# The last head of a differential-attention layer: the first output tile moved beside the first two score tiles, gates of that head kept on chip

## The chip, the cores and the metric

The kernel runs on one core of a Trainium2 chip. The metric is device time of one execution in microseconds (us). Three executions of the kernel before took 1778.83, 1778.11 and 1774.59 us; the median is 1778.11.

## What is computed

Two post-norm transformer layers over 1024 latent tokens of width 1024, with 256 context tokens as a prefix of the keys. Layer 0 is multi-head latent attention and is not touched. Layer 1 is differential attention with 8 heads: each head has two softmaxes over 1280 keys, and the second is taken off the first.

```python
def combine(o1, o2, gate):
    o = o1 - lam_full.astype(o1.dtype) * o2
    o = rms_norm(o, g_sub) * (1.0 - lambda_init)
    return gated(o, gate)                      # o * silu(gate)
...
o1, o1_c = prefix_attention(q[:, :, :, 0:1], k[:, :, :, 0], v, ...)
o2, o2_c = prefix_attention(q[:, :, :, 1:2], k[:, :, :, 1], v, ...)
...
x = layer_norm(DEEPNORM_ALPHA * x + gate[:, None, :] * (o @ out_w[i]), ln_g[i], ln_b[i])
```

The output is x after layer 1, so its projection with `out_w` and its LayerNorm end the kernel.

## The kernel before

Layer 1 works head by head, and each head in 8 row tiles of 128 tokens; one tile of one head is a step, written by `step1`. A step has three parts of three different tiles: the scores of tile t (`scores1`), the transposes of the combined probabilities of tile t-1 (`turn1`) and the values of tile t-2 (`values1`).

- `scores1` computes 128 x 1280 scores for both softmaxes in five PSUM banks of the eight ("b"), each by a pair of matmuls (L1347, L1348). DVE takes the negated maxima (`mx`, L1360 and L1364) and their minimum for each softmax (L1366). ACT writes the exponentials `p1` and `p0` (L1370), whose sums go through DVE (L1373 to L1375), and DVE combines both into one matrix (L1376).
- `turn1` transposes it on the PE (L1383, 4 + 4 + 2 blocks of 128) and splits each result into two fp16 parts: `ph` on ACT (L181), `pl` on DVE (L182).
- `values1` multiplies with the head's values in three passes (L1391 to L1393). ACT scales the result (L1396) and squares it (L1397), POOL makes the reciprocal root (L159, L160). For heads 0 to 6 POOL applies it (L1404) and SP stores the tile in DRAM, `o_d` (L1405). For the last head DVE multiplies by norm and gate in one instruction and writes the last 128 columns of `ws` (L1402).

Between these parts `step1` lets a second stream of PE work run, `side`, metered by five credits of a step (SLOT1, or SLOTO in the last head). PE's order is the written one (MAN1 is 'P'); the order of DVE, ACT, POOL and SP is made by a scheduler from readiness and priority. SP issues the DMAs and is one queue in order.

For heads 0 to 6 the second stream projects queries, keys, values and gates of the next head (`prod_q1`, `prod_k1`, `prod_v1`, `prod_w`). `prod_v1` ends by putting `top` on the list `later`: splitting the values, the SiLU of the gates in place and their store in DRAM, `sg_d`. Beside head 6 the stream is `v_last`: the projection of head 7's values and gates, interleaved with the preparation of `out_w`, whose eight blocks of 128 rows are kept as two fp32r parts each, `oHL`. `out_w1` prepares blocks 0 to 3; `out_pre` loads blocks 4 to 7 into `z` and `res` (L1450), scales the `res` ones on ACT (L1453) and all by the residual gate on POOL (L1454).

Head 7's second stream is the output projection. `out_open` loads ln_g into `wsq` (`gb2`), finishes the splits of blocks 4 to 7, and calls `out_load` for tiles 0 and 1. `out_load` brings a tile's 896 columns of heads 0 to 6 from `o_d` (L1482) and all its gates from `sg_d` (L1483), and POOL multiplies them (L1484). `out_turn` transposes blocks k = 0 to 6 of it (L1496) and splits them into `wx` (ACT, L176) and `wy` (DVE, L177); block 7 is there only after `values1`. `out_tile1` sums a tile in two banks, one for each half of 512 columns: 8 blocks of three matmuls (L185 to L187) each. The block k = 7 of both halves is last ("the close"); DVE adds the residual (L1531) and takes the statistics (L1532, L1535), POOL and ACT make the LayerNorm (L1545 to L1548; `wsq` is ln_g, `gb` ln_b), and SP stores the tile (L1549). The tile projected in step t is t-2. In steps 0 and 1 the second stream is empty, and two steps without scores follow step 7; I call them 8 and 9.

`w1(tag)` gives the next buffer of a tag: `ws` has three, `wx`, `wy`, `z` and `res` two, `wsq` one. A buffer that is given out again waits for the last reader of what it held.

Of the kernel before, what the change touches and what calls it, by code (L numbers as in the profile page):

```python
# [9 lines left out]
F32 = mybir.dt.float32  # L10
# [7 lines left out]
P = 128  # L18
# [17 lines left out]
NOW = 4  # L36
# [17 lines left out]
def hybrid_kernel(  # L54
# [994 lines left out]
    with ow_ctx, spool("o0") as op0:  # L1049
# [96 lines left out]
        for t in range(8):  # L1146
# [55 lines left out]
            "kr": ([P, NTOK], F32, 1), "kH": ([P, NTOK], F16, 1), "kL": ([P, NTOK], F16, 1)}  # L1202
    TAGV = {"rr": ([P, 512], F32, 1), "gg": ([P, SEQ // P, P], F32, 1), "Vf": ([P, NT, P], F32, 1)}

# [12 lines left out]
    oHL = [[wo4.tile([P, D], F32R, name=f"oH1{k}"), wo4.tile([P, D], F32R, name=f"oL1{k}")] for k in range(NOW)]  # L1217
    gate1 = wo4.tile([P, D], F32, name="gate1")
    wv1 = prv.enter_context(spool("a1projv", side="right"))
    for k_, v_ in TAGV.items():  # L1220
# [82 lines left out]
    def prod_v1(h):  # L1303
        w, uv = wt[1], un[1]
        gg, Vf = w1("gg"), w1("Vf")
        vt[h] = vh, vl = w1("vh"), w1("vl")
        vT = w1("rr")[:, :CTX]
# [26 lines left out]

        later.append(top)
        yield 0
# [50 lines left out]
    def values1(h, t, ph, pl, sm):  # L1387
# [11 lines left out]
        if h == H1 - 1:  # L1399
            oo, g = og[t]  # L1400
            c = slice(h * P, (h + 1) * P)
            dve.scalar_tensor_tensor(oo[:, c], o, ss[:, 1:2], g[:, c], op0=ALU.mult, op1=ALU.mult)  # L1402
            return
# [54 lines left out]
    def out_open():  # L1458

        prv.close()  # L1460
        wg1 = a1.enter_context(spool("a1outg"))
        place["g"] = wg1
        TAG1["g"] = ([P, D], F32, 2)
# [4 lines left out]
        out_load(0)  # L1468
        for k, w in enumerate(pre):
            if k % 2:  # L1470
                split(*oHL[NOW + k], w, e_lo=pool)
            else:
                act.activation(oHL[NOW + k][0], w, AF.Copy, scale=gsub)
                dve.scalar_tensor_tensor(oHL[NOW + k][1], w, gsub, fv(oHL[NOW + k][0]), op0=ALU.mult, op1=ALU.subtract)
            if k == 0:
                out_load(1)

    def out_load(t):

        ts = slice(t * P, (t + 1) * P)  # L1480
        o, g = og[t] = w1("ws"), w1("g")
        sp.dma_start(o[:, :DH], o_d[1][ts, :DH])  # L1482
        sp.dma_start(g, sg_d[1][ts, :])  # L1483
        pool.tensor_tensor(o[:, :DH], o[:, :DH], g[:, :DH], op=ALU.mult)  # L1484
# [3 lines left out]
    def out_turn(t, k0, n):  # L1488

        o, _ = og[t]  # L1490
        if k0 == 0:
# [15 lines left out]

    def out_tile1(t):

        ts = slice(t * P, (t + 1) * P)  # L1510
        tH, tL = oT[t]
        res = w1("res")
        sp.dma_start(res, zn_d[ts, :])
        y = [bank("b") for _ in range(2)]

        def mm(hh, k):
            c = slice(hh * 512, hh * 512 + 512)
            mm3(y[hh], tH[:, k, :], tL[:, k, :], oHL[k][0][:, c], oHL[k][1][:, c], k == 0, k == KT - 1)

        for hh in range(2):  # L1520
            for k in range(KT - 1):
                mm(hh, k)
                yield 1600
                if hh == 1 and k == 3:
                    out_turn(t, KT - 1, 1)
                    yield 256
        z, bs = w1("z"), w1("bs")
        for hh in range(2):
            mm(hh, KT - 1)
            c = slice(hh * 512, hh * 512 + 512)  # L1530
            dve.tensor_tensor(z[:, c], y[hh], res[:, c], op=ALU.add)  # L1531
            dve.bn_stats(bs[:, hh, :], z[:, c])  # L1532
# [31 lines left out]
    with tc.manual_schedule(engines={ENG[c] for c in MAN1}):  # L1564
# [38 lines left out]
        def v_last(h):  # L1603
            while later:
                later.pop(0)()
            out_early()
            yield from weave(prod_v1(h), chain(*[out_w1(k, lambda: w1("ws")) for k in range(NOW)],
                                               *[out_pre(k) for k in range(NOW, KT)]), range(1, 36, 2))

        g1 = gate_row1()  # L1610
        part = lambda h: (v for _, v in zip(range(4 if h else 0), g1))
        for h in range(H1):
# [5 lines left out]
            else:  # L1618
                while later:
                    later.pop(0)()  # L1620
                out_open()
            for t in range(SEQ // P):
                if last:
                    if t >= 2:
                        out_load(t)
                    G = weave(out_tile1(t - 2), out_turns(t - 1), (9, 12)) if t >= 2 else iter(())
                    if t == 2:
                        G = chain(out_turns(0), G)
                    credit[0] = 0
                step1((h, t), G, SLOT1 if not last else SLOTO)  # L1630
                if last:
                    for _ in G:
                        pass
            for _ in G:
                pass
        for t in range(SEQ // P - 2, SEQ // P):
            G = weave(out_tile1(t), out_turns(t + 1), (9, 12))
            credit[0] = 0
# [77 lines left out]
```

## Time and profile before

| | |
|---|---|
| median of three executions | 1778.11 us |
| profiled execution | 1777.68 us |
| its span in the profile | 1775.8 us (1.9 us lie around it) |
| mean granted clock of PE | 0.993 |
| PE busy | 1662.7 us, 94% |
| DVE, ACT, POOL busy | 69%, 63%, 46% |
| last head's steps 3 to 7 | 16.96 us each |

The span runs from the first to the last instruction, and times in the timelines count from its start. Head 7's first scores stand at about 1619 us, its last matmul ends at 1767, and the rest to 1775.8 is the last tile's LayerNorm and store. In a timeline a row has the start, the duration, the engine (SPq is SP's queue), the line, the operation, result and operands, and in brackets the idle time before it with what ended it. Rows of the waits give the total, how often and the longest. The granted clock is a share of full speed.

### The profile page before, as it was taken

Reading aid. Unit: us, or ns where it says so; the run is one execution under the profiler, and the core shown is the slowest. Engines: PE = TensorE matmul, PEld = TensorE weight load, DVE = VectorE, ACT = ScalarE, POOL = GpSimd, SP = SyncE. Lnnn points to the kernel's source line nnn. Section 1 sums busy time; section 2 is a strip of 40 time slices with the busy share of each in tenths; the row PEclk is TensorE's granted clock in tenths of the full one; section 3 lists DMA queues with packets and bytes.
Section 4 is the critical chain, followed back from the end, with each engine's and each line's share of the span. In section 5 each row is a group of like instructions: output and inputs, shape, how many; then the busy total and the mean of one; then the engine's idle time right before and its main releaser. Section 6 shows DMA issues by size and latency. Waiting matters only on the chain. (4 is left out here: it accounts for less than half of the span.)

```text
span 1775.8 us, 36794 instructions
## 1 busy us (share of the span) xinstructions
PE 1662.7 (94%) x14564; PEld 1232.4 (69%) x14564; DVE 1225.1 (69%) x2037; ACT 1117.2 (63%) x2235; POOL 822.2 (46%) x740
## 2 busy tenths in 40 slices
PE   7999999999999999899999999999999999988998
PEld 7999966556666565577867666767676757666876
DVE  7658675566665667646855778787877777878664
ACT  2551177677777777845635676767677766758542
POOL 1432147667777676846552323231414132455454
PEclk9999999999999999999999999999999999999999
DMA  8258520110111112155532213131312122241332
GB/s 302 85 151 258 165 69 22 41 45 21 42 46 28 37 55 69 57 176 187 166 101 61 78 54 80 55 81 55 79 43 69 41 57 62 66 127 67 109 111 71
DMA packets 111225, 154.84 MB, mean 87 GB/s; under 512 B 13415, under 2 KB 84679, under 8 KB 111054
## 3 DMA queue, kind: packets, MB, share of 16 engines
q1 hardware_dynamic: 102654, 144.90, 27.5%
q10 hardware_dynamic: 8400, 7.61, 1.3%
q8 instruction: 114, 1.87, 0.4%
q14 instruction: 57, 0.47, 0.1%
HBM read 98.65 MB, written 27.07 MB: 71 GB/s over the span
## 5 line engine op out<-in xcount | busy, mean ns | idle before, releaser
L779 POOL TENSOR_TENSOR pl<-p,ph 128x1024 f16<-128x1024 f32 (+1 forms) x176 | 365.4, 2082 | 150.0 <-ACT ph L778 123.4
L1370 ACT ACTIVATE p<-ps_b,mx 128x512 f32<-128x512 f32 (+1 forms) x384 | 230.2, 616 | 65.6 <-DVE mx L1366 64.6
L777 ACT ACTIVATE p<-ps_a,esc 128x1024 f32<-128x1024 f32 (+1 forms) x176 | 189.0, 1074 | 97.4 <-PE ps_a L835 91.3
L759 DVE TENSOR_REDUCE mx<-ps_a 128x1 f32<-128x1024 f32 x128 | 155.2, 1222 | 131.2 <-PE ps_a L757 131.1
L778 ACT CAST ph<-p 128x1024 f16<-128x1024 f32 (+1 forms) x176 | 177.1, 1006 | 5.5
L1364 DVE TENSOR_REDUCE mx<-ps_b 128x1 f32<-128x512 f32 x256 | 165.4, 680 | 0.4 <-PE ps_b L1348 0.3
L848 PE MATMUL ps_d<-Vh,pl 128*128 128x65 f16 x1344 | 146.6, 194 | 3.1 <-POOL pl L779 3.1
L845 PE MATMUL ps_d<-Vh,ph 128*128 128x65 f16 x1344 | 148.7, 195 | 0.0
L847 PE MATMUL ps_d<-Vl,ph 128*128 128x64 f16 x1344 | 147.5, 193 | 0.0
L845 PEld LDWEIGHTS <-ph 128*128 128x128 f16 x1344 | 123.7, 98 | 18.3 <-issue 5.2
L1347 PE MATMUL ps_b<-KS,QS 128*128 128x512 f16 (+1 forms) x384 | 126.5, 347 | 7.7 <-DVE pl L182 4.5
L847 PEld LDWEIGHTS <-ph 128*128 128x128 f16 x1344 | 124.3, 99 | 12.3 <-issue 0.5
L1395 POOL TENSOR_TENSOR sm<-sm,us 128x1 f32<-128x1 f32 x64 | 18.5, 288 | 245.9 <-DVE sm L1374 241.9
L833 PE MATMUL ps_a<-qH,KH 100*128 100x512 f16 x320 | 122.6, 383 | 9.1 <-ACT p L777 4.3
L1348 PE MATMUL ps_b<-KS,Q 128*128 128x512 f16 (+1 forms) x384 | 129.7, 347 | 0.0
L1383 PE MATMUL ps_b<-idr,p 128*128 128x128 f32 x640 | 102.7, 276 | 28.3 <-ACT rr L1313 7.8
L182 DVE SCALAR_TENSOR_TENSOR pl<-ps_b,lcf,ph 128x512 f16<-128x512 f32 (+1 forms) x192 | 116.8, 653 | 14.3 <-ACT ph L181 14.3
L848 PEld LDWEIGHTS <-pl 128*128 128x128 f16 x1344 | 123.5, 98 | 4.3 <-POOL pl L779 4.2
L181 ACT ACTIVATE ph<-ps_b,lcf 128x512 f16<-128x512 f32 (+1 forms) x192 | 115.4, 649 | 13.2 <-PE ps_b L1383 13.2
L834 PE MATMUL ps_a<-qH,KL 96*128 96x512 f16 x320 | 122.5, 383 | 0.0
L835 PE MATMUL ps_a<-qL,KH 96*128 96x512 f16 x320 | 121.9, 381 | 0.0
L1383 PEld LDWEIGHTS ps_b<-idr,p 128*128 128x128 f32 x640 | 77.0, 141 | 54.2 <-ACT p L1370 10.9
(438 smaller groups left out, 5293.6 us busy)
## 6 DMA issues: line engine op xcount, KB each, us to landing
ws<-in_dw SPq DMA_DIRECT2D x28, 512.0 KB, 4.1
adw<-in_ada_w SPq DMA_DIRECT2D x24, 512.0 KB, 4.7
adaw<-in_ada_w SPq DMA_DIRECT2D x16, 512.0 KB, 7.9
g<-sg_d SPq DMA_DIRECT2D x16, 512.0 KB, 9.1
sg_d<-gg ACTq DMA_DIRECT2D x40, 128.0 KB, 3.6
o_d<-op SPq DMA_DIRECT2D x7, 640.0 KB, 3.8
xt<-in_xT SPq DMA_DIRECT2D x16, 256.0 KB, 4.4
wgs<-in_w_in SPq DMA_DIRECT2D x32, 128.0 KB, 3.2
```

The source lines that it names most:

```text
L759: dve.tensor_reduce(mx[:, t, 0:1], ps, axis=AX.X, op=ALU.max)
L777: act.activation(p32[:, :n], st, AF.Exp, scale=esc0)
L778: act.copy(ph[:, :n], p32[:, :n])
L779: pool.tensor_tensor(pl[:, :n], p32[:, :n], ph[:, :n], op=ALU.subtract)
L845: pe.matmul(pv[:, t, :], ph[:, ts], Vh[:, k, h, :], start=(k == kcs[0] and t == 0), stop=False, skip_group_check=True)
L847: pe.matmul(pv[:, t, :V0], ph[:, ts], Vl[:, k, h, :], start=False, stop=False, skip_group_check=True)
L848: pe.matmul(pv[:, t, :], pl[:, ts], Vh[:, k, h, :], start=False, stop=(k == NT - 1), skip_group_check=True)
L1347: pe.matmul(out, qs[m][:, ts], ks[m][:, c0:c0 + n], start=True, stop=False)
L1348: pe.matmul(out, q1[m][:, ts], ks[m][:, c0:c0 + n], start=False, stop=True)
L1364: dve.tensor_reduce(mx[:, 2 + 2 * m + i:3 + 2 * m + i], b, axis=AX.X, op=ALU.max, negate=True)
L1370: act.activation(p[m][:, c0:c0 + n], b, AF.Exp, bias=nb, accum_out=sm[:, 2 + 3 * m + i:3 + 3 * m + i])
L1383: pe.transpose(st[:, j * P:(j + 1) * P], pc[:, (k0 + j) * P:(k0 + j + 1) * P], idn)
```

## The change

The changed file is longer, so lines move by 1 to 43; what was L1402 is L1408, L1366 is L1374, L1376 is L1384, L1404 and L1405 are L1410 and L1411, L1453 is L1459, L1482 to L1484 are L1496, L1499 and L1500, L1531 is L1570.

- Tile 0 is projected beside steps 0 and 1 of head 7: k = 0 to 3 of both halves in step 0, interleaved with the splits of `out_w` (`out_split`), k = 4 to 6 in step 1. Its two banks stay open until step 2.
- From step 2 on, the second half of tile s-2 and the first half of tile s-1 are computed, then the k = 7 transposes and close of tile s-2 (`out_step`, `out_close`). The transposes of tile s come behind that close.
- `out_first` loads tiles 0 and 1 in `v_last`, with gates in `wsq`; tile 0 is transposed at the end of `v_last`. ln_g takes `wsq` after them. Later tiles' gates go to the tag `gg`, which moves to a pool that stays.
- Head 7's values are split and its gates put through SiLU after step 1 (`out_gates`), into `g7` on chip. They aren't stored, and the loads of gates shrink to 896 columns.
- The credits of steps 0 and 1 are SLOTF.

```diff
 SLOTO = 0, 7000, 7000, 7000, 7000
+SLOTF = 0, 4800, 3200, 3200, 3200
...
@@ prod_v1
-        later.append(top)
+        if h < H1 - 1:
+            later.append(top)
+        else:
+            og.update(Vf=Vf, gg=gg, uv=uv)
@@ values1
-            dve.scalar_tensor_tensor(oo[:, c], o, ss[:, 1:2], g[:, c], op0=ALU.mult, op1=ALU.mult)
+            dve.scalar_tensor_tensor(og[t][:, DH:], o, ss[:, 1:2], og["g7"][:, t, :], op0=ALU.mult, op1=ALU.mult)
@@ out_load
-    def out_load(t):
+    def out_load(t, g_tag="gg"):
-        o, g = og[t] = w1("ws"), w1("g")
+        o, g = w1("ws"), w1(g_tag)
+        og[t] = o
         sp.dma_start(o[:, :DH], o_d[1][ts, :DH])
-        sp.dma_start(g, sg_d[1][ts, :])
+        sp.dma_start(g[:, :DH], sg_d[1][ts, :DH])
         pool.tensor_tensor(o[:, :DH], o[:, :DH], g[:, :DH], op=ALU.mult)
+    def out_gates():
+        vt[H1 - 1] = vh, vl = w1("vh"), w1("vl")
+        split16(vh, vl, og["Vf"], kc1)
+        prv.close()
+        wg1 = a1.enter_context(spool("a1outg", side="right"))
+        og["g7"] = wg1.tile(GG[0], GG[1], name="g7")
+        act.activation(flat(og["g7"]), flat(og["gg"]), AF.Silu, scale=og["uv"])
+    def out_mm(t, hh, ks):
+        for k in ks:
+            if k == 0:
+                oy[t, hh] = bank("b")
+            mm3(oy[t, hh], tH[:, k, :], tL[:, k, :], oHL[k][0][:, c], oHL[k][1][:, c], k == 0, k == KT - 1)
+            yield 1600
+    def out_step(s):
+        a, b = s - 2, s - 1
+        early, late_ = range(NOW), range(NOW, KT - 1)
+        if s == 0:
+            yield from weave(chain(out_mm(0, 0, early), out_mm(0, 1, early)), out_split(), (0, 2, 4, 6))
+            return
+        if s == 1:
+            yield from chain(out_mm(0, 0, late_), out_mm(0, 1, late_), out_turns(1))
+            return
...
+        if a:
+            yield from out_mm(a, 1, range(KT - 1))
+        if b <= end:
+            yield from out_mm(b, 0, early if a else range(KT - 1))
+        out_turn(a, KT - 1, 1)
+        yield 256
+        if a and b < end:
+            yield from out_mm(b, 0, late_)
+        yield from out_close(a, res)
+        yield from out_turns(s)
@@ v_last
             yield from weave(prod_v1(h), chain(*[out_w1(k, lambda: w1("ws")) for k in range(NOW)],
-                                               *[out_pre(k) for k in range(NOW, KT)]), range(1, 36, 2))
+                                               out_first(0), *[out_pre(k) for k in range(NOW, KT)],
+                                               out_first(1)), range(1, 36, 2))
+            yield from out_turns(0)
+        def out_first(t):
+            out_load(t, "wsq")
+            yield
```

What it does to the order of the queues stands below in three places. Numbers behind a name tell its uses apart.

First, SP's queue near the end of head 6, before: the stores and loads from the tiles in `o_d`, the last queries of head 7 (`QS`, `Q1`), then ln_b (`gb3`) and the blocks of `out_w`.

```order
L1482 DMA ws_3354_21996<-o_d1_100 128x896
L1482 DMA ws_3356_22003<-o_d1_100 128x896
L86 DMA QS0_3224_21118<-kH_3252_21275 64x512 x2
L86 DMA QS1_3225_21119<-kH_3252_21275 64x512
L86 DMA Q10_3222_21116<-kL_3253_21276 64x512 x2
L86 DMA QS1_3225_21119<-kH_3252_21275 64x512
L86 DMA Q11_3223_21117<-kL_3253_21276 64x512 x2
L1405 DMA o_d1_100<-o1_3272_21397 128x128
L966 DMA gb3_3254_21291<-in_ln_b 128x1024
L1450 DMA z_3305_21630<-in_out_w 128x1024
L1450 DMA res_3315_21691<-in_out_w 128x1024
```

The same place after:

```order
L1496 DMA ws_3305_21630<-o_d1_100 128x896
L1496 DMA ws_3351_21959<-o_d1_100 128x896
L1499 DMA wsq_3352_21960<-sg_d1_98 128x896
L87 DMA QS0_3224_21118<-kH_3252_21275 64x512 x2
L87 DMA Q10_3222_21116<-kL_3253_21276 64x512 x2
L87 DMA QS1_3225_21119<-kH_3252_21275 64x512 x2
L87 DMA Q11_3223_21117<-kL_3253_21276 64x512 x2
L967 DMA wsq_3359_22009<-in_ln_g 128x1024
L1411 DMA o_d1_100<-o1_3272_21397 128x128
L967 DMA gb3_3254_21291<-in_ln_b 128x1024
L1456 DMA z_3308_21652<-in_out_w 128x1024
L1456 DMA res_3323_21761<-in_out_w 128x1024
```

The load of tile 1's gates into `wsq` now stands ahead of the queries, and ln_g into the same `wsq` ahead of the store, of ln_b and of the blocks of `out_w`.

Second, POOL's queue at the same place, before: the last rotation work of head 7's queries (`rr`), then norms of head 6 (`ss`, `o1`) and the residual gate on `out_w`.

```order
L1245 TENSOR_TENSOR rr_3250_21269<-rr_3250_21269,rsw_3251_21270 128x512
L1395 TENSOR_TENSOR sm_3233_21153<-sm_3233_21153,us_2991_19668 128x1
L159 TENSOR_SCALAR ss_3274_21399<-ss_3274_21399 128x1
L160 TENSOR_TENSOR ss_3274_21399<-ss_3274_21399,neghalf_66 128x1
L1404 TENSOR_SCALAR o1_3272_21397<-o1_3272_21397,ss_3274_21399 128x128
L1395 TENSOR_TENSOR sm_3263_21318<-sm_3263_21318,us_2991_19668 128x1
L1454 TENSOR_TENSOR z_3305_21630<-z_3305_21630,gate1_12517 128x1024
L1454 TENSOR_TENSOR res_3315_21691<-res_3315_21691,gate1_12517 128x1024
```

After:

```order
L1249 TENSOR_TENSOR rr_3250_21269<-rr_3250_21269,rsw_3251_21270 128x512
L1500 TENSOR_TENSOR ws_3305_21630<-ws_3305_21630,wsq_3306_21631 128x896
L1403 TENSOR_TENSOR sm_3233_21153<-sm_3233_21153,us_2991_19668 128x1
L1500 TENSOR_TENSOR ws_3351_21959<-ws_3351_21959,wsq_3352_21960 128x896
L160 TENSOR_SCALAR ss_3274_21399<-ss_3274_21399 128x1
L161 TENSOR_TENSOR ss_3274_21399<-ss_3274_21399,neghalf_66 128x1
L1410 TENSOR_SCALAR o1_3272_21397<-o1_3272_21397,ss_3274_21399 128x128
L1403 TENSOR_TENSOR sm_3263_21318<-sm_3263_21318,us_2991_19668 128x1
L1460 TENSOR_TENSOR z_3308_21652<-z_3308_21652,gate1_12517 128x1024
L1460 TENSOR_TENSOR res_3323_21761<-res_3323_21761,gate1_12517 128x1024
```

The two products of tiles 0 and 1 (`ws`) come ahead of the norm whose result the store L1411 sends.

Third, DVE in one of the steps 3 to 7, from the statistics of an output tile (`bs`) on, before; `ws` is the normed and gated tile of head 7, `mx` the maxima.

```order
L1532 BN_STATS bs_3489_22775<-z_3488_22774 128x6 x2
L1364 TENSOR_REDUCE mx_3493_22804<-ps_b_3500_22826 128x1
L1535 BN_AGGR mv_3490_22786<-bs_3489_22775 128x2
L1360 TENSOR_REDUCE mx_3493_22804<-ps_b_3497_22808 128x2
L1364 TENSOR_REDUCE mx_3493_22804<-ps_b_3501_22830 128x1
L1364 TENSOR_REDUCE mx_3493_22804<-ps_b_3498_22814 128x1
L1366 TENSOR_SCALAR mx_3493_22804<-mx_3493_22804 128x1
L1364 TENSOR_REDUCE mx_3493_22804<-ps_b_3499_22818 128x1
L1366 TENSOR_SCALAR mx_3493_22804<-mx_3493_22804 128x1
L1402 SCALAR_TENSOR_TENSOR ws_3429_22419<-o1_3503_22869,ss_3505_22871,g_3430_22420 128x128
```

After:

```order
L1571 BN_STATS bs_3492_22799<-z_3491_22798 128x6 x2
L178 TENSOR_TENSOR wy_3495_22820<-ps_b_3496_22821,wx_3494_22819 128x512
L1574 BN_AGGR mv_3493_22810<-bs_3492_22799 128x2
L178 TENSOR_TENSOR wy_3495_22820<-ps_b_3497_22828,wx_3494_22819 128x384
L1372 TENSOR_REDUCE mx_3500_22843<-ps_b_3507_22865 128x1
L1368 TENSOR_REDUCE mx_3500_22843<-ps_b_3504_22847 128x2
L1372 TENSOR_REDUCE mx_3500_22843<-ps_b_3508_22869 128x1
L1372 TENSOR_REDUCE mx_3500_22843<-ps_b_3505_22853 128x1
L1374 TENSOR_SCALAR mx_3500_22843<-mx_3500_22843 128x1
L1372 TENSOR_REDUCE mx_3500_22843<-ps_b_3506_22857 128x1
L1408 SCALAR_TENSOR_TENSOR ws_3436_22458<-o1_3510_22908,ss_3512_22910,g7_22288 128x128
L1374 TENSOR_SCALAR mx_3500_22843<-mx_3500_22843 128x1
```

The splits `wy` of the next tile stand behind the statistics, and the write of `ws` (L1408, was L1402) stands ahead of the second negated maximum (L1374, was L1366), where before it stood behind both.

More of the change, by code (lines that the diff above doesn't have):

```diff
@@ L1218, in hybrid_kernel @@
     gate1 = wo4.tile([P, D], F32, name="gate1")
+    rot(wo4, GG[0], GG[1], "gg", GG[2], first=True)
+    place["gg"], TAG1["gg"] = wo4, GG
     wv1 = prv.enter_context(spool("a1projv", side="right"))
@@ L1305, in prod_v1 @@
         gg, Vf = w1("gg"), w1("Vf")
-        vt[h] = vh, vl = w1("vh"), w1("vl")
+        vh, vl = w1("vh"), w1("vl")
+        vt[h] = vh, vl
         vT = w1("rr")[:, :CTX]
@@ L1458, in out_open @@
     def out_open():
[L1460 to L1463, printed above, removed]
         og["gb2"] = w1("wsq")
@@ L1488, in out_turn @@
     def out_turn(t, k0, n):
-        o, _ = og[t]
+        o = og[t]
         if k0 == 0:
@@ L1506, in out_turns, with out_close @@
         yield 768
-    def out_tile1(t):
-        ts = slice(t * P, (t + 1) * P)
[L1511 to L1526, printed above, removed]
+    oy = {}
+    def out_mm(t, hh, ks):
+        tH, tL = oT[t]
+        c = slice(hh * 512, hh * 512 + 512)
+        for k in ks:
[12 more added lines that the diff above has]
+            return
+        res = w1("res")
+        sp.dma_start(res, zn_d[a * P:(a + 1) * P, :])
+        end = SEQ // P - 1
+        if a == end:
+            yield from out_mm(a, 0, late_)
+        if a:
[8 more added lines that the diff above has]
+        yield from out_turns(s)
+    def out_close(t, res):
+        ts = slice(t * P, (t + 1) * P)
         z, bs = w1("z"), w1("bs")
         for hh in range(2):
-            mm(hh, KT - 1)
+            for _ in out_mm(t, hh, (KT - 1,)):
+                pass
             c = slice(hh * 512, hh * 512 + 512)
-            dve.tensor_tensor(z[:, c], y[hh], res[:, c], op=ALU.add)
+            dve.tensor_tensor(z[:, c], oy[t, hh], res[:, c], op=ALU.add)
             dve.bn_stats(bs[:, hh, :], z[:, c])
@@ L1618, in hybrid_kernel @@
             else:
-                while later:
-                    later.pop(0)()
                 out_open()
@@ L1625, in hybrid_kernel @@
                         out_load(t)
-                    G = weave(out_tile1(t - 2), out_turns(t - 1), (9, 12)) if t >= 2 else iter(())
-                    if t == 2:
-                        G = chain(out_turns(0), G)
+                    G = out_step(t)
                     credit[0] = 0
-                step1((h, t), G, SLOT1 if not last else SLOTO)
+                step1((h, t), G, SLOT1 if not last else SLOTF if t < 2 else SLOTO)
                 if last:
@@ L1633, in hybrid_kernel @@
                         pass
+                    if t == 1:
+                        out_gates()
             for _ in G:
```

15 lines of the change are left out of this document (8 added, 7 removed).

## The prediction

> **What bounds the kernel now.** I read the page first, then busy time by stretches of ten microseconds over the region that the change touches, then what TensorE (PE) waits for there, then the timelines of the engines that it waits for.
>
> ```profile
> span 1775.8 us, 36794 instructions
> PE 1662.7 (94%) x14564; PEld 1232.4 (69%) x14564; DVE 1225.1 (69%) x2037; ACT 1117.2 (63%) x2235; POOL 822.2 (46%) x740
> ```
>
> PE is the bound on the whole. All sums below are made against the profiled execution: a span of 1775.8 us and 1777.68 us in all, 0.43 us under the median of 1778.11. The change adds no arithmetic, so it can only move PE's idle time, and what is worth having is read from the stretch around the start of the last head (columns: PE, weight loads, DVE, ACT, POOL, granted clock, DMA share, GB/s).
>
> ```profile
> 1600.00:1610.00 10.00, 10.00 (x101) 8.49 (x99) 7.57 (x15) 6.81 (x24) 2.44 (x4) 1.00 0.05 15
> 1620.00:1630.00 10.00, 4.47 (x14) 1.98 (x15) 8.67 (x14) 9.97 (x21) 6.97 (x3) 0.73 0.69 245
> 1625.00:1631.00 6.00, 5.47 (x20) 2.70 (x21) 4.55 (x8) 5.46 (x17) 4.35 (x3) 0.50 0.86 334
> 1630.00:1640.00 10.00, 8.22 (x89) 6.79 (x88) 8.27 (x19) 6.77 (x22) 6.82 (x10) 0.93 0.07 26
> 1700.00:1710.00 10.00, 10.00 (x76) 7.69 (x75) 9.89 (x20) 2.63 (x6) 3.31 (x5) 1.00 0.64 205
> ```
>
> From 1620 to 1640 PE stands and its clock falls to 0.73, while ACT is full. From 1640 to the end PE is full, but DVE is too (9.89 of 10). What PE waits for there (total, times, longest; then single matmuls with the wait ahead of them in brackets):
>
> ```profile
> PE ps_b L1383 <- DVE p L1376: 4.1, 3, 1.8
> ```
>
> ```profile
> 1589.75 0.66 PE L1383 MATMUL ps_b<-idr,p 128*128 128x128 f32 x4 [0.56 <-ACT p L1370]
> 1591.54 0.27 PE L185 MATMUL ps_b<-wx,h1H 128*128 128x256 f16 x1 [0.79 <-ACT p L1370]
> 1625.53 0.69 PE L1383 MATMUL ps_b<-idr,p 128*128 128x128 f32 x2 [5.83 <-DVE pl L182]
> 1626.99 0.63 PE L1347 MATMUL ps_b<-KS,QS 128*128 128x512 f16 x1
> 1656.06 0.38 PE L1347 MATMUL ps_b<-KS,QS 128*128 128x512 f16 x1
> ```
>
> The gap of 5.83 us is what output tile 0 is pulled forward to fill. Behind it the same score matmul starts 0.42 us after the one before and is shown with 0.63 us against 0.38, which is the lower clock.
>
> **1. The gain on offer.** The wait of 5.83, the longest of those for L1376 (1.8), about 0.9 of smaller ones, and the slow clock: from 1625 to 1631 the profile grants 0.50, which for 5.47 us of busy PE is 2.7 us. In all 11.2 us. That is the ceiling. But the gap is there because ACT is full (9.97 of 10) with splits, softmax and table work that stays, and the score banks come free by DVE's and ACT's work. With two of eight PSUM banks now held by tile 0's sums, steps 1 and 2 can't run their scores ahead. I expect step 3 to begin about when it does now, with the extra work done: 21 matmuls of tile 1 and 7 transposes. A matmul of the output projection starts every 0.23 us, from the rows
>
> ```profile
> 1764.43 0.40 PE L185 MATMUL ps_b<-o,wx 128*128 128x512 f32 x1
> ...
> 1766.50 0.39 PE L185 MATMUL ps_b<-o,wx 128*128 128x512 f32 x1
> ```
>
> (nine starts in 2.07 us), so 4.9 us and 0.8 us of transposes: **-5.7 us**, bounds 0 (the banks eat it) and -11.2 (all of it).
>
> **2. The load chain ahead of the head.** The order shows that SP's queue now has the gates of tile 1 behind the buffer of tile 0's gates, and the load of ln_g behind tile 1's, since `wsq` is a single buffer. SP is in order, and behind these two waits stand a store of the head before, ln_b and the four rows of out_w that ACT scales ahead of the softmax. Before, only the store waited for POOL, and for nothing but its own norm:
>
> ```profile
> 1572.05 1.53 SPq L1482 DMA_DIRECT2D ws<-o_d  x2
> ...
> 1579.02 1.42 SPq L1405 DMA_DIRECT2D o_d<-o  x1
> ...
> 1581.48 0.38 SPq L1450 DMA_DIRECT2D res<-in_out_w  x1
> ```
>
> ```profile
> g<-sg_d SPq DMA_DIRECT2D x16, 512.0 KB, 9.1
> DMA to landing us min/median/max: 3.9/4.2/8.4
> L1484 POOL TENSOR_TENSOR ws<-ws,g x8: 2081/2119/2835, 1628.7 to 1738.0; 128x896 f32<-128x896 f32 x8
> ```
>
> The first of these rows is of the loads of gates, both layers (median to landing), the second of the loads from o_d, the third of the gate products on POOL. After: tile 0's rows land at 1572.05 + 3.9 = 1576.0; product 0 ends at 1578.1; the gates of tile 1 are issued then and land at 1582.3 (4.2, as of a load from o_d of the same size in a quiet queue; the gates' own 9.1 was measured in a busy one and is the upper bound); product 1 ends at 1584.4. Only then ln_g goes out, and POOL's norm for the waiting store follows. Its three instructions take
>
> ```profile
> 1575.34 0.19 POOL L159 TENSOR_SCALAR ss<-ss 128x1 f32<-128x1 f32 x1 [0.85 <-ACT o L1397]
> 1575.61 1.75 POOL L160 TENSOR_TENSOR ss<-ss,neghalf 128x1 f32<-128x1 f32 x1
> 1577.46 0.61 POOL L1404 TENSOR_SCALAR o<-o,ss 128x128 f32<-128x128 f32 x1
> ```
>
> 2.7 us here, and 1.6 where L160 takes its usual 0.55 (row below); I take 1.6. So the store leaves at 1586.0, and with three issues of some 0.5 us the first `res` load at 1587.6 against 1581.48: 6.1 us late. Who waits for it:
>
> ```profile
> 1587.88 1.15 ACT L1453 ACTIVATE res<-res,gsub 128x1024 f32<-128x1024 f32 x1 [3.82 <-DMA res<-in_out_w]
> 1588.93 0.67 ACT L1370 ACTIVATE p<-ps_b,mx 128x512 f32<-128x512 f32 x1
> ```
>
> ACT already stands 3.82 us for this load, with the exponentials of a score tile right behind, and PE waits 0.56 and 0.79 us for those. All 6.1 us therefore reach PE, and PE, full from there on (10.00 in the row of 1600 to 1610), can't win it back: **+6.2 us**, bounds 0 (the loads are on time after all) and 11 (gates that land after 9.1). The new gap near 1590 is about 6.8 us, longer than the one of 5.83 that brought the clock to 0.50, so I charge the same loss less what falls into idle time: **+1.9 us**, bounds 0 and 3.
>
> The row of the 5.83 us gap carries that. The Trainium skill, TensorE: Matmul & The Clock Gate, Part 1, says that the clock halves after one idle window of about 3.4 us and comes back after as long a busy one; by that the loss would be 1.7 us and not 1.9 to 2.7, and waits under 3.4 us would be free. The trace differs in both: the slow stretch above lasted six microseconds, and a shorter stop did it too:
>
> ```profile
> 711.00:713.00 2.00, 0.03 (x1) 0.02 (x1) 1.99 (x2) 1.97 (x3) 0.96 (x1) 1.00 0.59 225
> ...
> 714.00:716.00 2.00, 2.00 (x6) 0.66 (x5) 0.43 (x4) 0.50 (x1) 2.00 (x2) 0.50 0.76 286
> ```
>
> **3. Steps 3 to 7: the loop through DVE.** A step takes 16.96 us, from one first score matmul to the next:
>
> ```profile
> 1654.75 0.28 PE L1347 MATMUL ps_b<-KS,QS 128*128 128x256 f16 x1
> ...
> 1671.71 0.28 PE L1347 MATMUL ps_b<-KS,QS 128*128 128x256 f16 x1
> ```
>
> PE is full, but beside it runs a loop of nearly the same length: output sums, z, statistics, the LayerNorm products on POOL, the head's norm behind them on POOL, L1402 on DVE, softmax combination, splits, k=7's split, k=7's matmuls, z again.
>
> ```profile
> 1656.75 0.68 DVE L1364 TENSOR_REDUCE mx<-ps_b 128x1 f32<-128x512 f32 x1
> 1657.34 0.20 DVE L1535 BATCH_NORM_AGGREGATE mv<-bs 128x2 f32<-128x12 f32 x1
> ...
> 1665.88 0.35 DVE L1402 SCALAR_TENSOR_TENSOR ws<-o,ss,g 128x128 f32<-128x128 f32 x1 [5.50 <-POOL ss L160]
> ...
> 1666.79 1.55 DVE L1376 SCALAR_TENSOR_TENSOR p<-p,sm,p 128x1280 f32<-128x1280 f32 x1
> ...
> 1669.58 1.34 DVE L177 TENSOR_TENSOR wy<-ps_b,wx 128x512 fp32r<-128x512 f32 x3
> ...
> 1671.23 1.36 DVE L1531 TENSOR_TENSOR z<-ps_b,res 128x512 f32<-128x512 f32 x2
> ```
>
> ```profile
> 1665.30 0.55 POOL L160 TENSOR_TENSOR ss<-ss,neghalf 128x1 f32<-128x1 f32 x1
> ```
>
> ```profile
> 1662.02 0.69 ACT L1370 ACTIVATE p<-ps_b,mx 128x512 f32<-128x512 f32 x1
> ...
> 1664.24 0.71 ACT L181 ACTIVATE ph<-ps_b,lcf 128x512 f16<-128x512 f32 x1
> ```
>
> The rows of DVE left out have no wait in brackets: its only stop in the step is the 5.50 us for POOL. Now the order puts the second negated maximum (L1374, was L1366) **behind** L1408 (was L1402). It feeds the last four exponentials, 1662.02 to 1664.24, which today run while DVE waits for POOL. In the new order they come after POOL: +2.2, and +0.27 for the maximum and some 0.1 of signals, 2.6 in the loop. Out of the loop go two of the three `wy` splits, now behind the statistics (1.25 becomes 0.3: -0.95), and one maximum ahead of the aggregation is replaced by a split (0.6 becomes 0.45: -0.15). The loop grows from at most 16.96 by 1.5 to about 18.4 us. Over five steps, of which the first starts with some room: **+6.5 us**, bounds 0 (the loop has slack that I don't see) and +8.
>
> **4. Steps 2, 8 and 9.** The single k=7 transpose now stands directly ahead of the k=7 matmuls, where no other work is left to put between. Before, nine matmuls (2.0 us) lay between and hid it. The cast of such a piece is
>
> ```profile
> 1667.89 0.27 ACT L176 CAST wx<-ps_b 128x128 fp32r<-128x128 f32 x1 [0.22 <-PE ps_b L1496]
> ```
>
> a wait of 0.22 and 0.27 us; with a like wait and some 0.3 for the split (three of them take 1.34 above), and a last signal to PE, about 1.2 us each time, an estimate from these rows; in step 8 besides the values wait for the last two transposes and L1408 for POOL's LayerNorm. Three times 1.2 and a little: **+3.8 us**, bounds +2 and +5. The gates kept on chip save transfers (a store and eight loads become smaller) that no PE wait above ends on; their Silu moves behind step 1 and takes, by L1453's row for the same size, 1.15 us of ACT, which lies within the bounds of part 1: 0.
>
> **Sum.** -5.7 + 6.2 + 1.9 + 6.5 + 3.8 = +12.7: 1777.68 + 12.7 = **1790 us**.
>
> **The rivals.**
> - *Only the load chain bites*: PE stays the pace of steps 3 to 7, for which its 10.00 in the row of 1700 to 1710 speaks. Without the 6.5: 1784 us. Against it: DVE is 9.89 busy in that row, and the moved maximum is in its queue.
> - *Only the loop bites*: ACT's res load is on time, as when the products come earlier than I think. Without 6.2 and 1.9: 1782 us. It is against the queue's order, in which product 0 needs rows that land at 1576.
> - *Faster*: the fill works in full at one place, 1619 to 1636, taking all 11.2 us; this wins if ln_g leaves SP's queue before about 1581 and the late exponentials fit into the loop's slack. With the low bound of 2 from part 4: 1777.7 - 11.2 + 2 = 1768.5, say 1769 us.
> - *The fill does not do what it says*: the two held banks stall steps 1 and 2 by as much as is filled. Term 1 is 0: 1796 us.
>
> **How the numbers follow.** Chances: forecast 0.50, load chain alone 0.17, loop alone 0.13, faster 0.12, no fill 0.08. A measurement of this kernel tells about 0.3% (5.3 us) from no change, so slower is above 1783.4 and faster below 1772.8. The forecast and the fill that fails are slower (0.58); the load chain alone lies on the edge (half of it, 0.09), the loop alone mostly within (0.04 slower). Slower 0.71, same 0.18, faster 0.11. The range leaves out the faster case and a little above: 1776 to 1798. The forecast's own is 1785 to 1796.
>
> **What would show it.** Load chain: SP waiting on POOL at L967 and L1411; ACT's L1459 waiting some 10 us for its DMA; a PE gap of 6 to 7 us near 1590 and a granted clock of 0.50 behind it. Loop: steps of 18.4 us in place of 16.96, with the p0 exponentials starting right behind DVE L1408 and PE waiting for `wy` ahead of k=7. Fill: no wait of 5.83 in step 1, and step 3 beginning near 1654.75 plus part 2. I am wrong if ACT's L1459 waits under 5 us, if the steps still take 17.0 us, or if step 3 begins more than 8 us from where these parts put it.

## The result, and the profile after

The changed kernel takes 1795.0 us in the median of four executions (1793.62 to 1799.05) against 1776.35 before; the ratio is 1.0111 with a 95% interval of 1.0099 to 1.0123. It is slower by about 20 us. The profiled execution, the fastest of the four, took 1793.62 us, 15.9 more than the profiled one of before, so the traces account for 16.0 us of span (1791.8 against 1775.8).

The page, first two lines and the shares of the chain that ended last, after; the last line is that chain before:

```profile
span 1791.8 us, 36791 instructions
PE 1667.8 (93%) x14564; PEld 1233.8 (69%) x14564; DVE 1225.5 (68%) x2037; ACT 1116.5 (62%) x2235; POOL 819.0 (46%) x740
...
DVE 3%; POOL 3%; ACT 1%; issue 1%; PE 0%; POOLq 0%; DVEq 0%
```

```profile
PE 7%; DVE 3%; ACT 1%; DMA 1%; POOL 1%; SPq 0%; issue 0%; POOLq 0%; DVEq 0%
```

This is the shortest sign of what changed: followed back from the last instruction, the chain now runs through DVE and POOL, where it ran through PE. Stretches and PE's waits after:

```profile
1590.00:1600.00 10.00, 6.33 (x30) 4.67 (x31) 3.79 (x6) 8.34 (x23) 8.05 (x5) 0.66 0.42 168
...
1620.00:1630.00 10.00, 10.00 (x82) 8.15 (x80) 9.30 (x14) 9.17 (x16) 5.61 (x4) 1.00 0.20 62
1630.00:1640.00 10.00, 8.40 (x65) 6.21 (x64) 8.81 (x16) 8.10 (x19) 3.40 (x7) 1.00 0.34 104
1640.00:1650.00 10.00, 7.30 (x52) 4.76 (x51) 6.33 (x12) 6.05 (x17) 2.58 (x3) 1.00 0.17 52
```

```profile
PE ps_b L188 <- DVE wy L178: 7.0, 6, 1.7
PE ps_b L1391 <- ACT p L1378: 4.6, 1, 4.6
PE ps_b L1355 <- DVE pl L183: 3.0, 3, 1.6
...
PE ps_b L1512 <- DVE ws L1408: 2.1, 2, 1.6
```

The gap of 5.83 us is filled (PE 10.00 from 1620 to 1630, clock 1.00). In its place stand a gap of 4.61 us near 1593 with the clock at 0.66, small waits up to 1650, and a wait for `wy` ahead of nearly every close. From the starts of each step's first score matmul in the two timelines (head 7's first stands at 1614.82 us before, not at 1619, which is where the gap of 5.83 us begins; after, it stands at 1621.39):

| stretch of the last two heads | before | after | |
|---|---|---|---|
| head 6, its step with the new gap | 12.90 | 19.78 | +6.9 |
| rest of head 6 | 20.45 | 21.21 | +0.8 |
| head 7, steps 0 to 2 | 39.93 | 40.28 | +0.3 |
| steps 3 to 6 | 67.84 | 76.28 | +8.4 |
| step 7, with steps 8 and 9, to the last matmul's end | 44.75 | 45.30 | +0.5 |

Unrounded that is 17.0 us; this stretch starts 1.1 us earlier than before (1580.40 against 1581.47) and the tail behind it is 0.1 longer, which makes the 16.0.

The load chain in SP's queue and at ACT, after:

```profile
1568.98 1.53 SPq L1496 DMA_DIRECT2D ws<-o_d  x2
1574.54 0.32 SPq L1499 DMA_DIRECT2D wsq<-sg_d  x1
...
1580.97 0.48 SPq L967 DMA_DIRECT2D wsq<-in_ln_g  x1
1583.72 0.33 SPq L1411 DMA_DIRECT2D o_d<-o  x1
...
1585.09 0.38 SPq L1456 DMA_DIRECT2D res<-in_out_w  x1
```

```profile
1591.34 1.15 ACT L1459 ACTIVATE res<-res,gsub 128x1024 f32<-128x1024 f32 x1 [8.35 <-DMA res<-in_out_w]
```

The two stops are there: 4.0 us without an issue ahead of the gates of tile 1, and 2.3 us between ln_g and the store. The first res load goes out 16.1 us behind the loads from `o_d`; before it was 9.4.

And the loop, in one of the steps 3 to 7 (DVE, then POOL, then ACT):

```profile
1709.63 0.35 DVE L1408 SCALAR_TENSOR_TENSOR ws<-o,ss,g 128x128 f32<-128x128 f32 x1 [4.88 <-POOL ss L161]
1709.90 0.27 DVE L1374 TENSOR_SCALAR mx<-mx 128x1 f32<-128x1 f32 x1
1712.59 0.16 DVE L1381 TENSOR_REDUCE sm<-sm 128x2 f32<-128x6 f32 x1 [2.42 <-ACT p L1378]
...
1713.24 1.55 DVE L1384 SCALAR_TENSOR_TENSOR p<-p,sm,p 128x1280 f32<-128x1280 f32 x1
...
1716.90 1.39 DVE L1570 TENSOR_TENSOR z<-ps_b,res 128x512 f32<-128x512 f32 x2 [0.20 <-PE ps_b L188]
```

```profile
1706.29 2.40 POOL L1587 TENSOR_TENSOR z<-z,gb 128x1024 f32<-128x1024 f32 x1
1708.77 0.19 POOL L160 TENSOR_SCALAR ss<-ss 128x1 f32<-128x1 f32 x1
1709.04 0.55 POOL L161 TENSOR_TENSOR ss<-ss,neghalf 128x1 f32<-128x1 f32 x1
```

```profile
1710.20 0.69 ACT L1378 ACTIVATE p<-ps_b,mx 128x512 f32<-128x512 f32 x1 [4.46 <-DVE mx L1374]
```

Read it as one line of dominoes: POOL's product, norm, DVE's L1408, the maximum behind it, the exponentials, then DVE waits 2.42 us for these. ACT stands 4.46 us with its scores ready, for an instruction of 0.27 us that stands in the wrong place of DVE's queue.

### The profile page after: what moved, and what is told of

It reads as the page before. It is cut to its first block, busy times and chain, and to the rows that moved or that the text cites. A ratio compares the mean times of both kernels' runs of the same rounds, so it can differ in the third digit from the quotient of the medians.

```text
span 1791.8 us, 36791 instructions
## 1 busy us (share of the span) xinstructions
PE 1667.8 (93%) x14564; PEld 1233.8 (69%) x14564; DVE 1225.5 (68%) x2037; ACT 1116.5 (62%) x2235; POOL 819.0 (46%) x740
## 5 line engine op out<-in xcount | busy, mean ns | idle before, releaser
L1403 POOL TENSOR_TENSOR sm<-sm,us 128x1 f32<-128x1 f32 x64 | 18.4, 287 | 257.6 <-DVE sm L1382 255.0
```

## The experiments

My theory: the load chain through `wsq` and the loop through DVE are two separate causes. The rivals: both are passing waits that come back elsewhere, and the fill itself (two banks held, PE's new order) costs the time. All times below are medians with the ratio to the kernel before, timed on the same chip, and its 95% interval. The kernel before had medians of 1776.1 to 1777.3 us in these comparisons, so medians of different rows compare only to about 1 us.

| kernel | us | ratio |
|---|---|---|
| changed | 1795.0 | 1.0111 (1.0099 to 1.0123) |
| gates_only | 1776.9 | 1.0001 (0.9982 to 1.0019) |
| early_loads | 1784.3 | 1.0051 (1.0033 to 1.0069) |
| chain_off | 1795.4 | 1.0103 (1.0069 to 1.0136) |
| loop_off | 1788.7 | 1.0062 (1.0039 to 1.0085) |
| both_off | 1788.9 | 1.0068 (1.0050 to 1.0085) |
| chain_off2 | 1790.1 | 1.0075 (1.0058 to 1.0092) |
| both_off2 | 1784.9 | 1.0042 (1.0027 to 1.0057) |
| no_fill | 1786.2 | 1.0056 (1.0039 to 1.0074) |
| tail_dve | 1780.1 | 1.0011 (1.0001 to 1.0021) |
| best | 1781.1 | 1.0025 (1.0015 to 1.0034) |
| final_z | 1780.9 | 1.0020 (1.0007 to 1.0033) |
| one_bank | 1775.7 | 0.9997 (0.9987 to 1.0006) |

### gates_only: one part alone

On the kernel before:

```diff
 def top():
             act.activation(g, g, AF.Silu, scale=uv)
+            if h == H1 - 1:
+                og["g7"] = gg
+                return
...
-        sp.dma_start(g, sg_d[1][ts, :])
+        sp.dma_start(g[:, :DH], sg_d[1][ts, :DH])
```

> The kernel before with one part of the change alone: head 7's gates stay on chip, are not stored, and the tiles' gate loads are 896 columns wide. My theory gives this nothing, within 2 us of the kernel before, since no wait of PE ends on these transfers. Rival, that the store and loads around 1620 to 1640 (245 GB/s) hold the start of the last head: 3 us or more faster.

1.0001: nothing that the interval of about 0.2% either way would show, so the smaller transfers don't explain the result.

### early_loads: the load chain alone

gates_only and, besides:

```diff
-            yield from weave(prod_v1(h), chain(..., *[out_pre(k) for k in range(NOW, KT)]), range(1, 36, 2))
+            yield from weave(prod_v1(h), chain(..., out_first(0), *[out_pre(k) for k in range(NOW, KT)],
+                                               out_first(1)), range(1, 36, 2))
```

with `out_load(0)` and `out_load(1)` gone from `out_open`.

> The kernel before with the gates kept on chip and, besides, only the early loads of tiles 0 and 1 into the one buffer with ln_g behind them: nothing of the output projection moves. If the load chain costs by itself: ACT waits 8 to 12 us for the res load, a PE wait of 4 to 9 us near 1593 with a slow clock behind it, and 1777 plus 6 to 9: some 1784 us. Rival, that the chain is harmful only with the projection pulled forward: within 2 us of 1777.

It took 7.4 us more than gates_only, and PE and ACT show why:

```profile
PE ps_b L1389 <- ACT p L1376: 8.8, 1, 8.8
PE ps_b L1389 <- DVE pl L182: 5.6, 1, 5.6
```

```profile
1593.73 1.15 ACT L1457 ACTIVATE res<-res,gsub 128x1024 f32<-128x1024 f32 x1 [12.04 <-DMA res<-in_out_w]
```

The chain costs by itself, with nothing of the projection moved; the long wait of before (5.83 us there, 5.6 here) is still there behind it.

### chain_off, chain_off2: the chain taken out of the changed kernel

```diff
 chain_off:
-                                               out_first(1)), range(1, 36, 2))
+                                               ), range(1, 36, 2))
...
+                    if t == 0:
+                        out_load(1, "z")
 chain_off2, besides:
-            out_load(t, "wsq")
+            out_load(t, "z")
```

> The changed kernel, but tile 1 is loaded behind step 0 of the last head with its gates in a buffer of z (free only then), so that in SP's queue neither tile 1's gates nor ln_g wait for a product on POOL. If the load chain is a cause of its own: ACT's wait for the res load of out_w falls from 8.35 to about 3.8 us, PE's wait of 4.61 us near 1593 to under 1 us, no slow clock there, and about 7 us less than the changed kernel: some 1788 us, with steps 3 to 7 still at 18.4 to 19.8 us. Rival, that the last head's own order sets the end and the late loads are only absorbed earlier: the same 4 us of wait come back at the next wait for ACT in steps 0 to 2, and the time stays within 2 us of 1795.

The first try failed to do what I meant: 1.0103. ln_g still took the single buffer behind tile 0's product, and SP stood 5.3 us ahead of it, with the queries behind it:

```profile
1572.00 1.54 SPq L1496 DMA_DIRECT2D ws<-o_d  x2
1578.87 0.33 SPq L967 DMA_DIRECT2D wsq<-in_ln_g  x1
...
1586.89 0.37 SPq L1456 DMA_DIRECT2D res<-in_out_w  x1
```

The res load was 14.9 us behind the loads, ACT waited 9.3 us. So this run tells nothing against either theory; it shows that one waiting issue is enough.

> The changed kernel, now with ln_g loaded into its buffer early as before the change, tile 0's gates in a buffer of z and tile 1's in another one behind step 0, so that SP waits for no product on POOL ahead of the res loads of out_w. In the first try ln_g still waited 5.3 us for tile 0's product, and the queries stood behind it. If the chain through the one buffer is the cause: the res load is issued some 10 us behind the loads from o_d (9.4 before, 16.1 in the changed kernel), ACT waits about 4 us for it, PE under 1.5 us near 1593 with the clock at 1.00, and the time is 6 to 8 us under 1795: 1788 us. Rival, that early loads cost by their traffic, not by the wait: the issue comes early, but the landing takes 10 us or more and PE waits as long as in the changed kernel.

With ln_g where it was before, the res load goes out 10.5 us behind the loads and ACT waits 5.27 us:

```profile
1569.26 1.53 SPq L1496 DMA_DIRECT2D ws<-o_d  x2
...
1579.71 0.38 SPq L1456 DMA_DIRECT2D res<-in_out_w  x1
```

1790.1 us, 4.9 under the changed kernel, less than the 6 to 8 expected. PE still waits 2.02 us near 1588, and that is enough for a slow clock (0.81 of full speed from 1590 to 1595; see the last section). ACT starts on the load 6.8 us behind its issue, against 6.4 before, so traffic is not the cause.

The edit also loses a part of what it wins. With tile 1 loaded behind step 0, head 7's step 1 takes 13.5 to 15.1 us (chain_off, chain_off2, both_off, both_off2), against 12.23 in the changed kernel and in loop_off, which load it early. chain_off and both_off have the late res load as well, so this is not the chain's wait coming back.

### loop_off, both_off, both_off2: the loop taken out

```diff
-            dve.scalar_tensor_tensor(og[t][:, DH:], o, ss[:, 1:2], og["g7"][:, t, :], op0=ALU.mult, op1=ALU.mult)
+            dve.tensor_tensor(og[t][:, DH:], o, og["g7"][:, t, :], op=ALU.mult)
+            pool.tensor_scalar(og[t][:, DH:], og[t][:, DH:], ss[:, 1:2], None, op0=ALU.mult)
```

> The changed kernel, but head 7's gate is multiplied on DVE ahead of the norm (it waits for ACT alone) and POOL applies the norm, so that no DVE instruction waits for POOL ahead of the second negated maximum. If the loop through DVE sets the steps: the last four exponentials start with the others, steps 3 to 7 fall from 19.0 to 17.0-17.3 us, PE's waits of 1.7 us for wy go, and the time is about 8 us less: some 1787 us. Rival, that the wait of PE for the k = 7 split comes from its place directly ahead of the close: steps stay above 18.4 us and the time within 2 us of 1795.

> Both edits together. If they are independent: 1795 less 7 and less 8, some 1780 us, and what is left against the 1776 of before are the k = 7 transposes without filler and the steps 0 to 2 that are no shorter. If the fill then shows its gain after all: 1770 us or less. If both undo the same time: no less than 1786.

> The same with the norm on POOL and the gate ahead of it on DVE, as in loop_off. If chain and loop are independent: 1788 less 6 to 8, some 1781 us, and steps 3 to 7 at 17.2 us. If less than 3 us under chain_off2: the two undo the same time.

loop_off: the steps fall from 19.0 to 17.21 us, PE's waits for `wy` ahead of the close are gone, and 1788.7 us are 6.3 under the changed kernel. That the wait comes from the transpose's place in PE's order is refuted: the place is unchanged. both_off has chain_off's flaw and stays at loop_off's time. both_off2 is 5.2 under chain_off2, so the two causes add up, though each is a little smaller than forecast.

### no_fill: what the fill is worth

```diff
-            yield from weave(chain(out_mm(0, 0, early), out_mm(0, 1, early)), out_split(), (0, 2, 4, 6))
+            yield from out_split()
...
-            yield from chain(out_mm(0, 0, late_), out_mm(0, 1, late_), out_turns(1))
+            yield from out_turns(1)
...
+        if not a:
+            yield from out_mm(a, 0, range(KT - 1))
```

> both_off2 with tile 0's 42 matmuls put back from steps 0 and 1 into step 2, all else as there. My term for the fill is 5.7 us, so this is 5 to 6 us slower than both_off2, with a PE gap of about 6 us and a slow clock in steps 0 and 1. If the fill is worth all that it promised: 10 us slower or more. If the held banks take back what it fills: within 2 us of both_off2.

1786.2 against 1784.9 for both_off2, and the intervals overlap: in the medians 42 matmuls (9.7 us at 0.23) moved into the gap bring 1.3 us, not the 5 to 6 expected. From step 0 to the start of step 3 the traces have 45.6 us without and 43.0 with the fill, and from step 0 to the last matmul's end 161.0 and 157.8, so the stage itself gains 3.2 us. Ahead of step 0 the profiled execution of no_fill was the faster one: its clock stayed at 1.00 near 1590, where that of both_off2 fell.

### tail_dve, best, final_z: where the lead is lost

tail_dve, on both_off2:

```diff
+        if t >= SEQ // P - 3:
+            dve.scalar_tensor_tensor(z, z, mv[:, 0:1], og["gb2"], op0=ALU.subtract, op1=ALU.mult)
+            dve.scalar_tensor_tensor(z, z, mv[:, 2:3], og["gb3"], op0=ALU.mult, op1=ALU.add)
+            sp.dma_start(out[ts, :], z)
+            yield 0
+            return
```

best also puts blocks 4 to 6 of the next tile's first half behind the k = 7 transpose in steps 2 and 8, final_z in step 8 alone.

> both_off2 with the LayerNorm of tiles 5 and 6 done by DVE (two instructions over 128x1024) in place of ACT and POOL, so that POOL's norm of the last two steps isn't behind their two products. both_off2 has 21 matmuls (4.9 us) less to do behind the start of step 7 than the kernel before and still takes 45.7 us for it against 44.75. If the fill's gain is lost in these two steps, to POOL's products ahead of the norm and to the slow clock that the wait brings: the waits of 0.82 and 1.83 us for the norm go, the last matmuls run at full clock, and it takes 41 to 42.5 us from step 7 to the last matmul: some 1781 us. Rival, that PE waits there for its own values and for the turn of k = 7 anyway: within 1.5 us of 1785.

From step 7 to the last matmul's end the kernel before takes 44.75 us, both_off2 45.72 and tail_dve 41.49 (in this order; the columns are those of the stretches above):

```profile
1722.59:1767.34 44.75, 44.75 (x284) 36.36 (x283) 21.45 (x43) 16.03 (x37) 22.40 (x24) 1.00 0.21 71
```

```profile
1729.34:1775.06 45.72, 41.59 (x257) 32.65 (x254) 21.46 (x42) 15.60 (x37) 24.36 (x26) 0.97 0.16 58
```

```profile
1730.01:1771.50 41.49, 40.01 (x257) 32.00 (x254) 26.46 (x46) 13.33 (x35) 18.40 (x20) 1.00 0.18 64
```

The waits of both_off2 for POOL's norm there were

```profile
PE ps_b L1513 <- POOL ws L1409: 2.7, 2, 1.8
```

and are gone; 1780.1 us, 4.8 less. PE waits for nothing in this stretch of the kernel before, so the edit takes back a cost of the change. Of the lead of 4.9 us in matmuls and 0.8 in transposes, 3.3 us now show; it was lost where POOL's two LayerNorm products of 2.4 us stand ahead of the last norm. In step 9 before, POOL made the norm (L160) ahead of the first product; in the changed kernel it makes it (L161) behind the second:

```profile
1758.30 0.55 POOL L160 TENSOR_TENSOR ss<-ss,neghalf 128x1 f32<-128x1 f32 x1
1759.31 2.41 POOL L1547 TENSOR_TENSOR z<-z,wsq 128x1024 f32<-128x1024 f32 x1 [0.46 <-ACT z L1546]
```

```profile
1777.53 2.38 POOL L1587 TENSOR_TENSOR z<-z,gb 128x1024 f32<-128x1024 f32 x1
1779.86 0.55 POOL L161 TENSOR_TENSOR ss<-ss,neghalf 128x1 f32<-128x1 f32 x1
```

> tail_dve, and in steps 2 and 8 too the blocks k = 4 to 6 of the next tile's first half go between the k = 7 transpose and its close, as filler. If the unfilled turn costs its 1.2 us in both, as forecast: 1 to 2.5 us under tail_dve, some 1779 us, still above the 1776.5 of before. If the filler only moves the wait to step 9: the same as tail_dve within 1 us.

> tail_dve with the filler behind the k = 7 transpose in step 8 alone, since in step 2 it brought the transpose ahead of POOL's norm (a wait of 3.38 us). From step 7 to the last matmul 40.7 us as in the kernel with both fillers, against 41.5 in tail_dve, and steps 0 to 3 as in tail_dve, 43.0: 0.8 us under tail_dve, some 1779 us. Rival: no difference that shows, within 0.5 us of 1780.

best takes 40.67 us at the end, 0.8 less, but in step 2 the earlier transpose waits 3.38 us for the norm: 1781.1, no gain. final_z has the end (40.70) without that wait and still measures 1780.9, so the 0.8 can't be told from noise.

### one_bank: the held banks

```diff
-            yield from weave(chain(out_mm(0, 0, early), out_mm(0, 1, early)), out_split(), (0, 2, 4, 6))
+            yield from weave(out_mm(0, 0, early), out_split(), (0, 1, 2, 3))
...
-            yield from chain(out_mm(0, 0, late_), out_mm(0, 1, late_), out_turns(1))
+            yield from chain(out_mm(0, 0, late_), out_turns(1))
...
-        if a:
-            yield from out_mm(a, 1, range(KT - 1))
+        yield from out_mm(a, 1, range(KT - 1))
```

> final_z with only the first half of tile 0 (21 matmuls, one held bank) in steps 0 and 1, the second in step 2. If the two held banks take back what the fill gives: the waits of 0.96 and 1.75 us for DVE's pl in step 1 go, steps 0 to 3 fall from 43.0 to 41.5 us or less although half as much is filled, and the time is 1.5 us or more under final_z. If DVE, full there (10.00 of 10 from 1620 to 1630), sets the pace: the 21 matmuls moved cost 2 to 5 us in step 2 and it is slower by that.

Half the fill with one held bank is 5.2 us faster than all of it with two, in the medians, and the two intervals just part; in the traces it is 2.5 us from step 0 on, all of it in steps 0 to 2 (40.9 us against 43.4). The waits of PE's score matmuls there, of final_z, then of one_bank:

```profile
PE ps_b L1355 <- DVE pl L183: 4.6, 4, 1.7
```

```profile
PE ps_b L1355 <- DVE pl L183: 1.7, 1, 1.7
PE ps_b L1355 <- ACT p L1378: 1.2, 1, 1.2
PE ps_b L1355 <- DVE wy L178: 0.8, 1, 0.8
...
PE ps_b L1355 <- DVE sm L1381: 0.4, 1, 0.4
```

In all they fall only from 4.6 to 4.1 us, and the wait of 1.7 us in step 1, which was to go if the held banks were the cause, stays. What goes lies in step 2: the values' wait of 1.25 us for `pl`, and waits of 0.51 and 0.87 us for the scaled values and the norm. There 21 matmuls more (4.8 us) make the step only 1.25 us longer (18.63 against 17.38), while steps 0 and 1 become 3.8 us shorter. So it is shown that the second half of tile 0 has a better place in step 2; that the held bank is the reason is not shown. With 0.9997 this version equals the kernel before; none of the versions beats it.

## Why the prediction was right

The forecast was 1790 us, 12.7 above the profiled execution of before; it became 15.9 there and about 20 in the ratio. Both mechanisms that made it slower were named, and runs that take each away alone get time back. The sum came out too low, above all by its terms 3 and 4. By its own steps:

1. **The fill, -5.7.** Up to step 3 it came as forecast: step 3 begins 40.28 us behind step 0 against 39.93 before, with the lead of 21 matmuls, and no_fill, which does the same work without the fill, though with tile 1 loaded later, needs 45.6. But behind step 7 there are 4.9 us of matmuls less, and it takes 0.5 us more; where the lead went stands under 4. The ceiling of 11.2 us was out of reach: in steps 0 to 2 PE still waits 6.0 us, 8.5 before. That the held banks are the reason, as I had argued, is not shown (one_bank).
2. **The load chain, +6.2 and +1.9.** The res load was 16.1 - 9.4 = 6.7 us later against 6.1 forecast, and the step with the gap 6.9 us longer against 8.1. The agreement is in part luck: in this profile SP reached the loads 1.5 us behind the start of their step, 3.0 before, which hid some of it; loop_off, with the same chain, had a PE wait of 8.86 us, and 22.34 us for that step. The price alone is 7.4 us (early_loads), 4.9 when taken away, and between loop_off and both_off2 that step falls by 6.9 us, of which step 1 of head 7 loses 2.8 again.
3. **The loop, +6.5.** It is +8.4 in four steps, just above the bound of 8 for five. The steps take 18.44, 19.02, 19.03 and 19.79 us; I had 18.4. By the rows of the step above: L1408 to the combination 3.61 us against 0.91 before (+2.70, forecast 2.6); from the combination to z 3.66 against 4.44 (-0.78, forecast -0.95); up to the aggregation nothing instead of -0.15; and POOL's `ss`, whose first instruction was between the two products and now comes behind them, +0.13. In the last of the four the clock also fell (0.50 near 1737). loop_off gives back 6.3 us.
4. **Steps 2, 8 and 9, +3.8: the term that was too small.** From step 7 on the forecast comes to -5.7 for the lead, +1.3 for the fifth step of the loop and some +2.6 for steps 8 and 9, -1.8 in all; measured is +0.5. I had priced the wait for POOL's norm there as "a little". tail_dve, which takes the products out of its way, makes the stretch 4.2 us shorter than both_off2, and 3.1 shorter than loop_off, whose clock stayed at 1.00 there (0.97 in both_off2). In the changed kernel it is mostly this wait ahead of the transpose, up to 1.60 us, and only 0.35 us of it the unfilled turn behind it; filler in step 8 saves 0.8 us in the traces and nothing that shows in the medians (final_z).
5. The clock: after the wait of 4.61 us it stood at 0.50 from 1593 to 1599, as after the 5.83 before, so the charge of 1.9 us was of the right kind.

Three rivals are out: that only the chain or only the loop bites (they add up in both_off2), and that the fill works in full. "The fill does not do what it says" gave 1796 us, nearer to the median of 1795.0 than my 1790. But its condition did not hold, since steps 0 to 2 took only 0.3 us more; the agreement in time does not speak for it.

Three things stay open. From the changed kernel to one_bank the medians fall by 4.9, 5.2, 4.8 and 4.4 us (chain_off2, both_off2, tail_dve, one_bank), but single executions of one kernel differ by up to 11 us, and I can't say which part that spread belongs to. Why final_z measures no better than tail_dve, with 0.8 us less at the end, was not settled. And with the loop out a step still takes 17.21 us and not 16.96, though PE waits for nothing in it.

## What to carry to other kernels

A buffer of one that two loads and a product share turns an in-order DMA queue into a chain: price everything that is queued behind the waiting issue, and take the buffer's later user away too, not only the first. When work is moved, look in the queues of the other engines for what the scheduler has put behind an instruction that waits for a third engine; here 0.27 us of DVE behind such a wait cost 2 us a step. And a lead won early must be followed to the last instruction: it is worth only what the last stage doesn't wait for anyway.

## What the runs showed of the hardware

**The clock falls after shorter waits than 5 us, and not always.** In both_off2 waits of 1.55 and 0.80 us with 1.0 us of work between them were enough:

```profile
1591.00:1592.00 1.00, 0.31 (x2) 0.25 (x2) 0.00 (x0) 1.00 (x3) 1.00 (x1) 0.76 0.97 397
1592.00:1593.00 1.00, 1.00 (x7) 0.67 (x6) 0.17 (x2) 1.00 (x5) 1.00 (x2) 0.50 0.92 374
```

In no_fill the same two waits (1.53 and 0.80) left it at 1.00:

```profile
1589.00:1590.00 1.00, 1.00 (x10) 0.89 (x10) 0.00 (x0) 1.00 (x5) 1.00 (x2) 1.00 0.98 395
```

The Trainium skill, TensorE: Matmul & The Clock Gate, Part 1, calls the window that is watched free-running, which fits a result that depends on when the wait falls; the idle window of about 3.4 us that it asks for was not needed here. Head 7's step 1 shows the same: behind waits of about 1.0 and 1.75 us the clock fell to 0.50 for some 3 us in both_off2 and stayed at 1.00 in chain_off2, and the step took 15.06 and 13.56 us.

**DVE and POOL slow each other.** The same combination on DVE and the same gate product on POOL overlap in two kernels; in the changed one DVE pays, in chain_off POOL does:

```profile
1572.50 3.35 DVE L1384 SCALAR_TENSOR_TENSOR p<-p,sm,p 128x1280 f32<-128x1280 f32 x1
```

```profile
1575.35 1.54 DVE L1384 SCALAR_TENSOR_TENSOR p<-p,sm,p 128x1280 f32<-128x1280 f32 x1
```

```profile
1575.51 3.33 POOL L1500 TENSOR_TENSOR ws<-ws,wsq 128x896 f32<-128x896 f32 x1 [3.00 <-DVE mx L1372]
```

POOL's product takes 2.08 us in the changed kernel. One is late by 1.3 to 1.8 us, about the rest of the other's instruction, whichever came second. The Trainium skill, SBUF — State Buffer, Who interferes with whom, says that a DVE instruction with two SBUF inputs contends with a GpSimd (POOL) instruction that reads SBUF for a shared port pair, and that the second to issue is blocked until the first is done; the rows agree. In loop_off DVE's gate, a 128x128 product that starts 0.85 us into POOL's LayerNorm product of 2.40, took 1.70 us and ended with it (at 1709.3); in step 2, with no POOL product beside it, the same instruction took 0.28 us.
